# The first stage of a hybrid decoder step: conditioning weights in whole rows, and a shift that is added apart

## The chip, the cores and the metric

The kernel runs on one core of a Trainium2 chip. The metric is the device time of one execution in microseconds (us); a shorter time is better. The engines of the core are named as in the profile: PE is TensorE (PEld its weight loads), DVE is VectorE, ACT is ScalarE, POOL is GpSimd, SP is SyncE, which issues most DMAs.

## What is computed

The reference is one inference step of a one-layer decoder trunk with width 1024, for a prompt of 512 tokens and 8 sample sequences of one token each. The 520 tokens are columns of one batch. What concerns the first stage:

```python
cs = silu(c)                                    # 9 conditioning vectors: prompt, 8 samples
mod = cs @ w_mod + b_mod                        # (9, 6 * 1024)
sh1, sc1, g1, sh2, sc2, g2 = split(mod, 6)
h = rmsnorm(x, norm1_g) * (1 + sc1) + sh1
u = h @ w_in                                    # 1024 x 8192
qa, fa, ia, oga, xb, yb, ga, gb = split(u)
...                                             # HGRN2 heads, RG-LRU, merge, w_out, MLP, final norm
```

Each token's scale and shift depend on its conditioning vector: one for all 512 prompt tokens, one for each sample. All is float32.

## The kernel before

Activations lie transposed: `h` is 8 tiles (k = 0 to 7) of 128 features by 520 tokens. To keep float32 accuracy, each matrix product is made from three fast products: an operand is split into a high part (a rounding copy, on ACT) and a low part (the rest, a subtraction on DVE), and PE adds high x high, high x low, low x high. One weight tile of 1024 x 128 is thus 8 (k) x 3 x 2 (halves of 260 tokens) = 48 products in `products` (L115). `gemm` makes them, `take_w` fetches the tile: it keeps loads (`_load_w`, L66, buffers "wst", four of them) and splits (`_split_w`, L75 and L78) some tiles ahead. Float32 products without a split (w_mod's, for instance) stand as two passes in the trace.

`run` lists the weight tiles in order. Head 0 of the HGRN2 part needs four: f, q, g and v (kf, kq, kg, kv). The first two are multiplied in `begin`, which is the first stage; the rest follow in `head`.

`begin` loads the conditioning vectors and x (L393, 512 KB for 128 tokens, rows of 4 KB). It then loads w_mod's scale and shift columns for each k as one tile "wm" of 1024 x 256 (L1432, two loads of 512 KB each, in runs of 512 B). The first two weight tiles go between. For each k, `mod` multiplies the 9 conditioning vectors with that tile (L356, in four groups of 32 columns of the array), copies the result out (L358), turns it (L372), and adds up the groups and the bias (L376, L380) into `modT`. `norm_x` and `scale_x` normalise x by rows; `transposed` turns 128 features at a time (L426) and ACT puts the result back (L427). `affine_split` forms `h[k]`, with scale and shift at once: the high part on ACT (L447), the full value and the low part on DVE (L448, L449), the samples on POOL (L443 to L445). Products of the f and q tiles with `h[k]` follow as each k is ready.

Small parameters are loaded as rows and turned by PE: `transpose_in` takes a tile "ps" in PSUM (the memory that PE writes to), transposes into it (L222), and DVE copies it out (L223). There are two "ps" tiles. `parameters_mod_in` does one such turn, `parameters_in` four.

The order of instructions on an engine is made by a scheduler at build time, from priorities (the order in the code) and estimated times: an instruction whose inputs or buffer aren't ready can be passed by a later one. `behind` and `issue_after` add an order by hand, with no wait of their own. At run time each engine takes its instructions in the order so fixed.

Of the kernel before, what the change touches and what calls it, by code (L numbers as in the profile page):

```python
# [6 lines left out]
F32 = mybir.dt.float32  # L7
# [26 lines left out]
LEAD = 4  # L34
# [13 lines left out]

class Kernel:
    def __init__(self, ctx, tc, ins, outs):  # L50
        self.ctx, self.tc, self.nc = ctx, tc, tc.nc
        self.i, self.o = ins, outs
        self.group, self.sigmoids, self.mod_open = None, [], None
        self.ppt_free = True
# [14 lines left out]
    def _split_w(self, st, place, after=None):  # L69
# [6 lines left out]
        if after:  # L76
            self.behind(ins, after)
# [9 lines left out]
    def load_split(self, key, stage):  # L87
        return self._split_w(self._load_w(key, stage), self.split_place())

    def take_w(self, key):  # L90
# [7 lines left out]
        while self.wnext_split < min(last + 1, len(self.wspecs)):  # L98
            while self.wnext_load < min(self.wnext_split + LOADS, len(self.wspecs)):
                self.wstage[self.wnext_load] = self._load_w(self.wspecs[self.wnext_load], self.wst)  # L100
                self.wnext_load += 1
# [4 lines left out]
        self.wcur += 1  # L106
        return self.wsplit.pop(n)

    def products(self, ps, w, a, first, last, extra=0, halves=(0, 1), after=None):

        (wh, wl), (ah, al) = w, a
        for n, (x, y) in enumerate(((wh, ah), (wh, al), (wl, ah))):
            for s in halves:
                c = slice(s * HALF, (s + 1) * HALF + s * extra)
                self.last_product = self.nc.tensor.matmul(ps[:, s, :c.stop - c.start], x, y[:, c],  # L115
# [4 lines left out]
    def gemm(self, keys, acts, extra=0):  # L120

        ps = self.pmm.tile([128, 2, 512], F32, name="mm")
        for q, key in enumerate(keys):
            hi, lo = self.take_w(key)
            for k in range(KO):
                n = q * KO + k
                self.products(ps, (hi[:, k], lo[:, k]), acts[n], n == 0, n == len(keys) * KO - 1, extra)
                if self.mod_open and k == MODK:
                    self.mod_close(self.last_product)
# [52 lines left out]
    def identity(self):  # L182
        nc, sb = self.nc, self.consts
        jp = self.start.tile([128, 128], I32, name="pi")
        nc.gpsimd.iota(jp, pattern=[[1, 128]], base=0, channel_multiplier=-1)
        self.ident = sb.tile([128, 128], F32, name="ident")
        nc.vector.tensor_scalar(self.ident, jp, 0.0, None, OP.is_equal)
        one = self.start.tile([128, 128], F32, name="ti")
# [6 lines left out]
    def constants(self):  # L195
        nc, sb = self.nc, self.hc

        pi = self.start.tile([128, NC, 32], I32, name="pi")
        ti = self.start.tile([128, NC, 32], I32, name="ti")
        nc.gpsimd.iota(pi, pattern=[[0, NC], [0, 32]], base=0, channel_multiplier=1)  # L200
        nc.gpsimd.iota(ti, pattern=[[0, NC], [1, 32]], base=0, channel_multiplier=0)
# [26 lines left out]
    def bounds(self):  # L228

        nc = self.nc  # L230
        r = self.start.tile([16, 128], F32, name="ra")
        nc.gpsimd.dma_start(r[0:8], self.rows8(self.i["hg_lower"]))
        nc.gpsimd.dma_start(r[8:16], self.rows8(self.i["lru_lambda"]))
# [11 lines left out]
        nc.scalar.activation(e, e, AF.Exp)  # L245
        self.exps = nc.scalar.activation(ex, na, AF.Exp)
# [6 lines left out]
        self.decay = ex, s, s2, acc, d  # L253

    def decays(self):

        nc = self.nc
        ex, s, s2, acc, d = self.decay
# [13 lines left out]
    def parameters_mod(self):  # L272

        r = self.start.tile([64, 128], F32, name="ra")
        for a, b, name in ((0, 48, "b_mod"), (48, 56, "norm1_g"), (56, 64, "norm2_g")):
            self.nc.sync.dma_start(r[a:b], self.rows8(self.i[name]))
# [70 lines left out]
    def mod(self, keys, w=None):  # L347
# [3 lines left out]
        w = w or self.take_w(self.mod_key(*keys[0]))  # L351
# [6 lines left out]
        first = nc.scalar.copy(ev[:, :n], ps[:, :n])  # L358
        self.mod_open = ev, keys
        if self.ppt_free:  # L360
            self.mod_close()
        return first

    def mod_close(self, after=None):
# [4 lines left out]
        pool, name = (self.ppt, "pt") if self.ppt_free else (self.pps, "ps")  # L369
        pt = pool.tile([128, 512], F32, name=name)  # L370
        for j in range(len(keys)):
            ins = nc.tensor.transpose(pt[:, j * 128:(j + 1) * 128], ev[:, j * 128:(j + 1) * 128], self.ident)  # L372
            if after:
                self.behind(ins, after)
# [3 lines left out]
        for j, (part, k) in enumerate(keys):  # L378
            g = (self.n1g if part == 1 else self.n2g)[:, k:k + 1] if part in (1, 4) else None
# [14 lines left out]

    def norm_x(self):
        nc = self.nc
        ss = self.sm.tile([128, 16], F32, name="ss")
        nc.vector.memset(ss, 1.0)
        junk = lambda: self.pmm.tile([128, 2, 512], F32, name="mm").rearrange("p a b -> p (a b)")
        j = junk()  # L400
        nc.vector.tensor_tensor(j[:NB], self.xsn, self.xsn, OP.mult)
        nc.vector.tensor_reduce(ss[:NB, NC:NC + 1], j[:NB], mybir.AxisListType.X, OP.add)
        for t in range(NC):
            last = nc.scalar.activation(junk(), self.xn[:, t], AF.Square, accum_out=ss[:, t:t + 1])
        self.behind(nc.scalar.activation(self.act0, self.act0, AF.Sigmoid), last)
        ss = ss[:, 0:8]
        nc.vector.tensor_scalar(ss, ss, 1.0 / D, EPS, OP.mult, OP.add)
        self.rs1 = self.rsqrt_small(ss, 8)

# [10 lines left out]
    def transposed(self, k):  # L420

        nc = self.nc
        ps = self.ppb.tile([128, 512], F32, name="pb")
        x = self.xn[:, :, k * 128:(k + 1) * 128]
        for t in range(NC):
            nc.tensor.transpose(ps[:, t * 128:(t + 1) * 128], x[:, t], self.ident)  # L426
        nc.scalar.copy(x, ps.rearrange("p (t f) -> p t f", f=128))  # L427
        return x

    def transposed_s(self):  # L430
# [4 lines left out]
        return ps  # L435
# [1104 lines left out]
```

## Time and profile before

| what | value |
|---|---|
| time, median of three runs | 1045.49 us (1044.67 to 1045.71) |
| the profiled execution's own time | 1044.54 us |
| its span, first to last instruction | 1042.6 us |
| PE, PEld | 1005.1 us, 968.5 us busy (96%, 93%) |
| DVE, ACT, POOL | 694.9, 526.1, 112.8 us busy |
| mean granted clock of TensorE | 0.996 |
| loads by SP's queue (hardware queue) | 130.28 MB, 44.1% of 16 engines' span |

The span is what the profile covers; the execution's own time is 1.94 us more. Busy time is the union of an engine's instructions. Windows give the busy time of each engine in a stretch, with the granted clock, the share in which the 16 DMA engines were busy, and GB/s. The chain of waits follows the work that ended last back to what released it.

### The profile page before, as it was taken

Reading aid. Unit: us, or ns where it says so; the run is one execution under the profiler, and the core shown is the slowest. Engines: PE = TensorE matmul, PEld = TensorE weight load, DVE = VectorE, ACT = ScalarE, POOL = GpSimd, SP = SyncE. Lnnn points to the kernel's source line nnn. Section 1 sums busy time; section 2 is a strip of 40 time slices with the busy share of each in tenths; the row PEclk is TensorE's granted clock in tenths of the full one; section 3 lists DMA queues with packets and bytes.
Section 4 is the critical chain, followed back from the end, with each engine's and each line's share of the span. In section 5 each row is a group of like instructions: output and inputs, shape, how many; then the busy total and the mean of one; then the engine's idle time right before and its main releaser. Section 6 shows DMA issues by size and latency. Waiting matters only on the chain.

```text
span 1042.6 us, 24269 instructions
## 1 busy us (share of the span) xinstructions
PE 1005.1 (96%) x9940; PEld 968.5 (93%) x9940; DVE 694.9 (67%) x1583; ACT 526.1 (50%) x1020; POOL 112.8 (11%) x215
## 2 busy tenths in 40 slices
PE   2999999999999999999999999999999999999995
PEld 1799999999999999989999999999999999999994
DVE  7558688695867768465333337767767676777775
ACT  5445753573574456342122224366555655656653
POOL 2200000000000000020000000011422231232040
PEclk9999999999999999999999999999999999999998
DMA  9963344343434324496555578332572484274242
GB/s 277 260 178 107 110 134 115 112 136 114 126 116 126 113 82 135 137 312 178 163 157 157 157 217 234 93 97 67 124 181 70 100 174 125 52 158 96 62 81 83
DMA packets 247792, 143.71 MB, mean 138 GB/s; under 512 B 6622, under 2 KB 242326, under 8 KB 247674
## 3 DMA queue, kind: packets, MB, share of 16 engines
q1 hardware_dynamic: 237874, 130.28, 44.1%
q0 software_dynamic: 9808, 11.89, 6.3%
q8 instruction: 78, 1.28, 0.5%
q14 instruction: 32, 0.26, 0.1%
HBM read 123.61 MB, written 11.26 MB: 129 GB/s over the span
## 4 chain that ended last, share of the span: by engine, by line
PE 90%; DMA 3%; SPq 3%; ACT 1%; DVE 1%; issue 1%; DVEq 0%; ACTq 0%
PE mm L115 65%; PE ps L1085 8%; PE pt L1085 4%; PE pb L1085 2%; PE ps L356 2%; SPq L1432 2%; PE pb L702 1%; PE ps L561 1%; DMA wst<-in_w_branch_a_dram 1%; DMA wst<-in_w_in_dram 1%; DMA wm<-in_w_mod_dram 1%; PE mm L1085 1%; PE pt L645 1%; PE pt L634 1%; PE ps L529 1%
## 5 line engine op out<-in xcount | busy, mean ns | idle before, releaser
L115 PE MATMUL mm<-h,whi 128*128 128x260 f32 (+1 forms) x3072 | 513.9, 286 | 1.4 <-ACT X L137 1.4
L115 PEld LDWEIGHTS mm<-h,whi 128*128 128x128 f32 x3072 | 427.3, 188 | 7.0 <-issue 3.4
L115 PE MATMUL mm<-h,wlo 128*128 128x260 f32 (+1 forms) x1536 | 316.4, 285 | 0.0
L75 ACT CAST whi<-wst 128x1024 fp32r<-128x1024 f32 x168 | 175.8, 1048 | 228.9 <-PE mm L115 175.4
L78 DVE TENSOR_TENSOR wlo<-wst,whi 128x1024 fp32r<-128x1024 f32 x168 | 205.1, 1222 | 91.2 <-ACT whi L75 90.1
L115 PEld LDWEIGHTS mm<-h,wlo 128*128 128x128 f32 x1536 | 240.0, 189 | 1.5 <-issue 1.0
L115 PE MATMUL mm<-a,whi 128*128 128x260 f32 x512 | 84.6, 285 | 0.0
L115 PEld LDWEIGHTS mm<-a,whi 128*128 128x128 f32 x512 | 70.6, 188 | 1.4 <-issue 1.4
L115 PE MATMUL mm<-a,wlo 128*128 128x260 f32 x256 | 52.3, 284 | 0.0
L797 POOL DMA_DIRECT2D t<-oaT_d x8 | 4.3, 550 | 399.2 <-ACT ma L137 389.0
L1181 DVE TENSOR_TENSOR f<-f 128x260 f32<-128x260 f32 x64 | 27.3, 427 | 28.3 <-ACT f L1176 27.6
L1170 ACT ACTIVATE ft<-ft,fsh 128x512 f32<-128x512 f32 (+2 forms) x36 | 24.0, 676 | 36.0 <-DVE ft L1167 36.0
L115 PE MATMUL mm<-b,whi 128*128 128x260 f32 x256 | 41.8, 285 | 0.0
L1173 POOL TENSOR_TENSOR ft<-ft,fsh 128x8 f32<-128x8 f32 x28 | 17.6, 629 | 219.0 <-DVE ft L1167 219.0
L115 PEld LDWEIGHTS mm<-a,wlo 128*128 128x128 f32 x256 | 39.5, 188 | 0.2 <-issue 0.2
L115 PEld LDWEIGHTS mm<-b,whi 128*128 128x128 f32 x256 | 35.0, 188 | 1.6 <-issue 1.6
L1215 POOL DMA_DIRECT2D ma<-snap x28 | 27.2, 971 | 35.2 <-issue 30.9
L1197 POOL DMA_DIRECT2D ma<-snap x28 | 26.2, 935 | 43.6 <-DMA ma<-snap 28.1
L813 DVE TENSOR_TENSOR t<-mm,t 128x520 f32<-128x520 f32 x8 | 5.6, 700 | 36.7 <-PE ps L372 36.7
L1176 ACT ACTIVATE f<-ft 128x520 f32<-128x520 f32 (+1 forms) x36 | 20.8, 587 | 14.4 <-POOL ft L1174 12.3
L376 DVE TENSOR_REDUCE mods<-ps 128x9 f32<-128x36 f32 x32 | 6.1, 192 | 31.4 <-PE ps L372 31.3
L115 PE MATMUL mm<-b,wlo 128*128 128x260 f32 x128 | 25.9, 283 | 0.0
(488 smaller groups left out, 1876.4 us busy)
## 6 DMA issues: line engine op xcount, KB each, us to landing
wst<-in_w_in_dram SPq DMA_DIRECT2D x64, 512.0 KB
wst<-in_w_mod_dram SPq DMA_DIRECT2D x32, 512.0 KB
wst<-in_w_ff_dram SPq DMA_DIRECT2D x64, 256.0 KB
wst<-in_w_ff_dram SPq DMA_DIRECT2D x32, 512.0 KB
wm<-in_w_mod_dram SPq DMA_DIRECT2D x16, 512.0 KB
st<-in_state_hgrn_dram SPq DMA_DIRECT2D x8, 512.0 KB
vb<-vd SPq DMA_DIRECT2D x8, 512.0 KB
out_dram<-st SPq DMA_DIRECT2D x8, 512.0 KB
```

Source lines behind the costliest of these rows:

```text
L75: ins = self.nc.scalar.copy(hi, st)
L78: self.nc.vector.tensor_tensor(lo, st, hi.bitcast(F32), OP.subtract)
L115: self.last_product = self.nc.tensor.matmul(ps[:, s, :c.stop - c.start], x, y[:, c], start=first and n == 0, stop=last and n == 2)
L356: nc.tensor.matmul(ps[r:r + 32, :n], self.cT[:, k, :], w[:, k, :], start=k < 4, stop=k >= KO - 4)
L1085: ins = self.nc.tensor.matmul(ps, x[:, w], y[:, f], start=j in (1, 7, 2) and k == 0 and n == 0, stop=k == 3 and n == 2, skip_group_check=True)
L1170: nc.scalar.activation(t[:, :p], t[:, :p], AF.Relu, bias=sh[:, 0:1])
L1173: eng.tensor_tensor(t[:, p:], t[:, p:], sh[:, 1:9], OP.add)
L1176: nc.scalar.activation(f, self.two(self.ft)[:, a:a + n], AF.Square)
L1181: self.nc.vector.tensor_tensor(f[:, n], f[:, a], f[:, b], op)
L1197: nc.gpsimd.dma_start(x[1][:, b], v[:, :n], accum_op=OP.add)
L1215: nc.gpsimd.dma_start(x[t][:, a], s[p], accum_op=OP.add)
L1432: nc.sync.dma_start(raw[k][:, :, j * 128:(j + 1) * 128], w[r:r + 1024, c:c + 128].rearrange("(k p) n -> p k n", p=128))
```

## The change

It concerns `begin` and what it calls; the stages behind it keep their code.

- w_mod is loaded in whole rows: `load_rows` takes 128 rows of 1024 columns (4 KB each), first the eight row tiles of the scale, later the eight of the shift in the same eight buffers. `mod_rows` adds up the conditioning product of each row tile in one PSUM tile, `mod_out` copies it out, `mod_cols` turns it and adds the bias, for all eight k at once.
- The first three weight tiles of head 0 (f, q, g) are loaded and split in `begin`, in buffers of their own, and multiplied with `h` as scaled only, without the shift (`scaled`, `rest`).
- The shift's share of these three tiles, shift x weights for 9 conditioning vectors, is a small product (`pw`), which is split (`shw`) and added to the three sums by a product with an indicator matrix (`shifted`, `indicator`): 9 rows spread to 520 tokens. Afterwards `h` is formed a second time, with the shift (`again`), for all later tiles.
- While `begin` runs, each instruction on PE, ACT and DVE is chained behind the one before it on its engine (`InOrder`), so that these three engines follow the order of the code. SP and POOL are not chained.
- `ready_w(1, 1)` loads and splits the v tile's weights before the products, and v's product goes to the PSUM tiles "pt" and "pb". Later weight splits stand behind the last of `again` on ACT (`start_act`).
- The loads of b_mod and the norm weights move from SP's to POOL's queue; the iotas and small parameter loads move ahead.

```diff
--- before.py
+++ after.py
-LEAD = 4
+FIRSTS = 3
...
+class InOrder:
...
+        def __getattr__(self, name):
+            fn = getattr(self.engine, name)
+            def call(*a, **kw):
+                ins = fn(*a, **kw)
+                if self.last:
+                    self.tc.add_manual_dep(ins.ins, self.last.ins.name, NOSYNC, reason="order")
+                self.last = ins
+                return ins
+            return call
...
-        if after:
-            self.behind(ins, after)
+        if after or self.start_act:
+            self.behind(ins, after or self.start_act)
...
+    def ready_w(self, end, loads=LOADS):
+        while self.wnext_split < min(end, len(self.wspecs)):
+            while self.wnext_load < min(self.wnext_split + loads, len(self.wspecs)):
                 self.wstage[self.wnext_load] = self._load_w(self.wspecs[self.wnext_load], self.wst)
                 self.wnext_load += 1
             st = self.wstage.pop(self.wnext_split)
             spec = self.wspecs[self.wnext_split]
             self.wsplit[self.wnext_split] = st if WHOLE in spec else self._split_w(st, self.split_place())
             self.wnext_split += 1
...
+        r = self.start.tile([64, 128], F32, name="rm")
         for a, b, name in ((0, 48, "b_mod"), (48, 56, "norm1_g"), (56, 64, "norm2_g")):
-            self.nc.sync.dma_start(r[a:b], self.rows8(self.i[name]))
+            self.nc.gpsimd.dma_start(r[a:b], self.rows8(self.i[name]))
         return r
...
+    def load_rows(self, part, k, t=None):
+        t = t or self.start.tile([128, D], F32, name="wm", bufs=NWM)
+        self.nc.sync.dma_start(t, self.i["w_mod"][0, k * 128:(k + 1) * 128, part * D:(part + 1) * D])
+        return t
+    def mod_rows(self, ps, k, w):
+        for j in range(4):
+            self.nc.tensor.matmul(ps[32 * j:32 * j + 32, :256], self.cT[:, k, :], w[:, 256 * j:256 * j + 256],
+                                  start=k == 0, stop=k == KO - 1)
+    def mod_out(self, ps):
+        ev = self.sm.tile([128, 256], F32, name="modev")
+        self.nc.scalar.copy(ev, ps[:, :256])
+        return ev
+    def mod_cols(self, part, out, ev, scale=None):
+        nc = self.nc
+        pt = self.ppb.tile([128, 512], F32, name="pb")
+        own = self.ident.rearrange("p (j c) -> p j c", c=32)[:, :, :NM]
+        for h in range(2):
+            nc.tensor.matmul(pt[:, 64 * h:64 * h + 4 * NM].rearrange("p (j b) -> p j b", b=NM),
+                             ev[:, 128 * h:128 * h + 128], own, start=True, stop=True)
+        src = pt[:, :128].rearrange("p (h x) -> p h x", h=2)[:, :, :4 * NM].rearrange("p h (j b) -> p h j b", b=NM)
+        out = out.rearrange("p (j h) b -> p h j b", h=2)
+        col = lambda c: c.rearrange("p (j h) -> p h j", h=2)[:, :, :, None].to_broadcast([128, 2, 4, NM])
+        nc.vector.tensor_tensor(out, src, col(self.bmod[:, part * 8:part * 8 + 8]), OP.add)
+        if scale is not None:
+            nc.vector.tensor_tensor(out, out, col(scale), OP.mult)
...
-        return nc.vector.tensor_tensor(lo, f, hi.bitcast(F32), OP.subtract)
+        hi, x = self.h[k][0], self.xcols(k)
+        f = self.start.tile([128, L], F32, name="ht", bufs=2)
+        if shift:
+            ins = nc.scalar.activation(v(hi), x, AF.Identity, bias=sh, scale=sc)
+            nc.vector.tensor_scalar(v(f), x, sc, sh, OP.mult, OP.add)
+        else:
+            ins = nc.scalar.activation(v(hi), x, AF.Copy, scale=sc)
+            nc.vector.tensor_scalar(v(f), x, sc, None, OP.mult)
+        return k, f, ins
+    def rest(self, t):
+        (hi, lo), f = self.h[t[0]], t[1]
+        return self.nc.vector.tensor_tensor(lo[:, :L], f, hi[:, :L].bitcast(F32), OP.subtract)
...
+            parts = list(zip((self.two(og)[:, s] for s in range(2)), first[2]))
+        else:
+            parts = [(self.two(og), self.gemm(kg, self.h)[:, :, :HALF])]
         with self.urgent():
-            self.sigmoid(self.two(og), ps)
...
-        ps = self.gemm(kv, self.h)[:, :, :HALF]
         v = self.slot(self.hg, "e")
+        if first:
+            ps = self.gemm(kv, self.h, ps=[self.ppt.tile([128, 512], F32, name="pt"),
+                                           self.ppb.tile([128, 512], F32, name="pb")], after=self.last_product)
+            parts = [(self.two(v)[:, s], ps[s][:, :HALF]) for s in range(2)]
+        else:
...
             kf, kq, kv, kg = self.head_cols(h)
-            steps.append(([kf, kq, kg, kv][2 if h == 0 else 0:], self.head_start if h == 0 else self.head, h))
+            steps.append(([kf, kq, kg, kv][FIRSTS if h == 0 else 0:], self.head_start if h == 0 else self.head, h))
...
     def begin(self):
...
+        plain = self.nc
+        nc = self.nc = InOrder(self.tc)
         self.start = self.open_pool("start", 1)
+        mm = lambda: self.pmm.tile([128, 2, 512], F32, name="mm")
...
+        rb, rm, par = self.load_bounds(), self.parameters_mod(), self.parameters()
+        rows = [self.start.tile([128, D], F32, name="wm", bufs=NWM) for _ in range(KO)]
         self.load_x()
+        keys = [self.head_cols(0)[j] for j in (0, 1, 3)]
+        raw = [self._load_w(keys[0], self.wst)]
+        rows = [self.load_rows(1, k, t) for k, t in enumerate(rows)]
+        raw += [self._load_w(key, self.wst) for key in keys[1:]]
+        first = []
+        def split_first(n):
+            hi, lo = (self.start.tile([128, KO, 128], F32R, name=x, bufs=FIRSTS) for x in ("fhi", "flo"))
+            nc.scalar.copy(hi, raw[n])
+            first.append((hi, lo))
+        def split_rest(n):
+            hi, lo = first[n]
+            nc.vector.tensor_tensor(lo, raw[n], hi.bitcast(F32), OP.subtract)
+        self.constants()
         self.cond()
...
+        self.norm_samples()
+        self.bounds(rb)
+        last = self.norm_x()
+        self.exponentials()
+        self.behind(nc.scalar.activation(self.act0, self.act0, AF.Sigmoid), last)
+        split_first(0)
+        self.scale_x()
+        self.shp = self.start.tile([128, KO, 32], F32, name="shp")
+        nc.vector.memset(self.shp, 0.0)
         hi, lo = (self.act.tile([128, KO, T2], F32R, tag="h", name="h", bufs=2) for _ in range(2))
         self.h = [(hi[:, k, :T], lo[:, k, :T]) for k in range(KO)]
...
+        psc = self.ppt.tile([128, 512], F32, name="pt")
+        for k in range(4):
+            self.mod_rows(psc, k, rows[k])
+        split_rest(0)
+        self.parameters_mod_in(rm)
+        t = self.transposed(0, 2, mm())
+        self.put_back(nc.scalar.copy, t)
+        self.mod_rows(psc, 4, rows[4])
+        t = self.transposed(2, 2, mm())
+        self.put_back(nc.vector.tensor_copy, t)
+        self.mod_rows(psc, 5, rows[5])
+        xs = self.transposed_s()
+        t = self.transposed(4, 1, ps()[:, None])
+        self.put_back(nc.scalar.copy, t)
+        self.mod_rows(psc, 6, rows[6])
+        t = self.transposed(5, 1, ps()[:, None])
+        self.put_back(nc.vector.tensor_copy, t)
+        self.mod_rows(psc, 7, rows[7])
+        ev = self.mod_out(psc)
+        last_x = [self.transposed(6, 1, ps()[:, None])]
+        self.mod_cols(1, self.modT[:, 8:16], ev, self.n1g)
+        last_x.append(self.transposed(7, 1, ps()[:, None]))
+        rows = [self.load_rows(0, k) for k in range(KO)]
+        fs = self.start.tile([128, KO, NB], F32, name="fs")
+        t = self.scaled(0)
+        nc.vector.tensor_tensor(fs, xs, self.modT[:, 8:16, 1:9], OP.mult)
+        nc.vector.tensor_copy(hi[:, :, L:T], fs)
+        nc.vector.tensor_tensor(lo[:, :, L:T], fs, hi[:, :, L:T].bitcast(F32), OP.subtract)
+        self.rest(t)
+        split_first(1)
+        t = self.scaled(1)
+        split_rest(1)
+        self.rest(t)
+        split_first(2)
+        for x in last_x:
+            self.put_back(nc.scalar.copy, x)
+        t = self.scaled(2)
+        split_rest(2)
+        self.rest(t)
+        for k in range(3, KO):
+            self.rest(self.scaled(k))
+        self.indicator()
+        self.ready_w(1, 1)
         self.parameters_in(*par)
...
+        self.decays()
+        self.first = [mm()[:, :, :HALF], mm()[:, :, :HALF], [ps()[:, :HALF], ps()[:, :HALF]]]
+        acc = [[x[:, s] for s in range(2)] for x in self.first[:2]] + [self.first[2]]
+        def products(n, *ks):
+            wh, wl = first[n]
+            for k in ks:
+                ah, al = self.h[k]
+                for m, (x, y) in enumerate(((wh, ah), (wh, al), (wl, ah))):
+                    for s in range(2):
+                        nc.tensor.matmul(acc[n][s], x[:, k], y[:, s * HALF:(s + 1) * HALF], start=k == 0 and m == 0,
+                                         stop=n < 2 and k == KO - 1 and m == 2)
+        def shifted(n):
+            for m, x in enumerate(shw):
+                for s in range(2):
+                    nc.tensor.matmul(acc[n][s], x[:, n * 128:(n + 1) * 128], self.ind[:, s * HALF:(s + 1) * HALF],
+                                     start=False, stop=n == 2 and m == 1)
+        def again(*ks):
+            for k in ks:
+                t = self.scaled(k, True)
+                plain.gpsimd.tensor_copy(hi[:, k, L:T], fs[:, k])
+                plain.gpsimd.tensor_tensor(lo[:, k, L:T], fs[:, k], hi[:, k, L:T].bitcast(F32), OP.subtract)
+                self.split_last, self.start_act = self.rest(t), t[2]
+        for k in (0, 1):
+            products(0, k)
+            products(1, k)
+        products(2, 0, 1)
+        for k in (2, 3):
+            for n in range(FIRSTS):
+                products(n, k)
+        psh = self.ppt.tile([128, 512], F32, name="pt")
+        for k in range(4):
+            self.mod_rows(psh, k, rows[k])
+        for n in range(FIRSTS):
+            products(n, 4)
+        for k in range(4, KO):
+            self.mod_rows(psh, k, rows[k])
+        ev = self.mod_out(psh)
+        for n in range(FIRSTS):
+            products(n, 5)
+        self.mod_cols(0, self.shp[:, :, :NM], ev)
+        plain.gpsimd.tensor_tensor(fs, fs, self.shp[:, :, 1:9], OP.add)
+        again(0, 1, 2)
+        products(0, 6)
+        products(1, 6)
+        pw = self.ppt.tile([128, 512], F32, name="pt")
+        for n in range(FIRSTS):
+            for k in range(KO):
+                r = 32 * (k % 4)
+                nc.tensor.matmul(pw[r:r + 32, n * 128:(n + 1) * 128], self.shp[:, k, :], raw[n][:, k, :],
+                                 start=k < 4, stop=k >= KO - 4)
+        shw = [self.start.tile([128, FIRSTS * 128], F32R, name=f"shw{x}") for x in "hl"]
+        nc.scalar.copy(shw[0], pw[:, :FIRSTS * 128])
+        nc.vector.tensor_tensor(shw[1], pw[:, :FIRSTS * 128], shw[0].bitcast(F32), OP.subtract)
+        products(2, 6, 7)
+        shifted(0)
+        products(0, 7)
+        shifted(1)
+        products(1, 7)
+        shifted(2)
+        again(*range(3, KO))
+        self.last_product = nc.tensor.last
+        self.nc = plain
...
+        _, _, p, n = self.counts
+        nc.vector.tensor_scalar(p, p, 31, None, OP.bitwise_and)
+        b = self.start.tile([128, 1], F32, name="ind_b")
+        nc.vector.tensor_copy(b, p)
+        self.ind = self.start.tile([128, T], F32R, name="ind")
+        nc.vector.tensor_scalar(self.ind, n, 0.0, b, OP.max, OP.is_equal)
...
```

206 lines of the change are left out of this document (91 added, 115 removed).

## The prediction

> **What bounds the kernel now.** I read the page first (busy shares and slices), then the windows of the first 60 us, then the chain of waits through them, then the engines' own order of instructions there.
>
> ```profile
> span 1042.6 us, 24269 instructions
> PE 1005.1 (96%) x9940; PEld 968.5 (93%) x9940; DVE 694.9 (67%) x1583; ACT 526.1 (50%) x1020; POOL 112.8 (11%) x215
> ```
>
> TensorE (PE) is busy for all but 37.5 us of the span. The windows (busy us and instructions of PE, PEld, DVE, ACT, POOL; granted clock; DMA share; GB/s) say where those are:
>
> ```profile
> 0.00:10.00 10.00, 1.24 (x9) 1.10 (x9) 6.28 (x33) 5.42 (x12) 6.50 (x17) 1.00 0.75 257
> 10.00:20.00 10.00, 2.97 (x20) 1.24 (x20) 6.86 (x40) 4.42 (x7) 0.00 (x0) 1.00 1.19 290
> 20.00:30.00 10.00, 6.55 (x67) 3.78 (x69) 5.87 (x20) 7.38 (x12) 0.00 (x0) 1.00 1.21 289
> 30.00:40.00 10.00, 8.47 (x94) 6.34 (x86) 6.68 (x16) 5.35 (x10) 4.24 (x15) 1.00 1.21 291
> 54.27:60.13 5.86, 5.86 (x48) 5.86 (x49) 5.76 (x18) 4.35 (x12) 0.00 (x0) 1.00 1.07 287
> 60.13:100.00 39.87, 39.87 (x492) 38.19 (x491) 29.32 (x77) 17.61 (x35) 0.00 (x0) 1.00 0.37 108
> ...
> 4.00:9.00 5.00, 0.48 (x4) 0.31 (x3) 4.24 (x19) 3.42 (x8) 3.45 (x8) 1.00 1.01 391
> ```
>
> In the first 40 us PE idles 20.8 us (40 less 1.24, 2.97, 6.55 and 8.47) while the DMA share is at or over 1 from 10 us on: the stage is bound by loads. From 54.27 on PE runs without a gap. The last row is the one stretch in which the queue moves mainly x, in rows of 4 KB: 391 GB/s against 290 in the stretches that load weight tiles in runs of 512 B. The chain of waits (start, us, what) names the same thing:
>
> ```profile
> 29.16 7.62 DMA wm<-in_w_mod_dram
> 36.78 0.14 issue
> 36.91 1.07 PE ps L356 x16
> ...
> 53.62 0.61 ACT X L137
> 54.23 0.04 issue
> 54.27 15.62 PE mm L115 x128
> ```
>
> So the place to compare is the end of the third weight tile of head 0 (its gate column, kg), after which either kernel goes on with the same work (kv, rg_x, ...) on a full PE. A 128x260 product costs 15.62 / 128 = 0.122 us there, and the third tile's 48 end at 54.27 + 48 x 0.122 = **60.1**: the 48 instructions of the window row that ends at 60.13. What the change is worth is the shift of this point.
>
> **The change, part by part.** The loads come first. x is seen complete by the last Square (9.95, below). Behind it now lie one weight tile, 0.52 MB at 290 GB/s = 1.8 us, and the eight scale rows, 4.19 MB. Nothing in the trace loads w_mod by rows; the x row bounds it from above (391 GB/s, 10.7 us), the tile rows from below (290, 14.5 us). I take 391, since a row here is the same 128 runs of 4 KB. The last scale row lands at 9.95 + 1.8 + 10.7 = 22.5.
>
> ```profile
> 9.95 1.03 ACT L404 ACTIVATE mm<-xn 128x1024 f32<-128x1024 f32 x1 [0.48 <-DMA xn<-in_x_prompt_dram]
> 26.98 0.37 ACT L358 COPY modev<-ps 128x256 f32<-128x256 f32 x1 [0.36 <-PE ps L356]
> 28.05 0.23 DVE L376 TENSOR_REDUCE mods<-pt 128x18 f32<-128x72 f32 x1 [2.15 <-PE pt L372]
> 28.32 0.42 DVE L380 TENSOR_SCALAR modT<-mods,pm 128x9 f32<-128x9 f32 x2
> 41.29 0.38 PE L372 MATMUL pt<-ident,modev 128*128 128x128 f32 x2
> 49.24 0.42 DVE L380 TENSOR_SCALAR modT<-mods,pm 128x9 f32<-128x9 f32 x2
> ```
>
> Its four products are 8 passes, half of 1.07 us; evacuation, turn and addition take 28.74 - 26.98 = 1.76 as above (the new form drops the reduce and adds a wider pass; bounds 1.4 to 2). All scales stand at **24.8**, where before the last column's scale came at 49.66 by the same steps. So far the change gains much.
>
> What decides is the order. Every PE, ACT and DVE instruction of the new begin() is chained to the one before on its engine. After the two transposes 6 and 7 and the turn of the scales, PE's next instructions are the four transposes of parameters_in, and only then the first product. They write to "ps" tiles, of which there are two. The third needs the first one's copy on DVE. That copy stands in DVE's order behind all eight scaled/rest pairs, the indicator, and the low half of the kv weight (ready_w). So the third transpose waits for all of that, and every product waits behind it on PE, though h[0] is ready early. The trace shows both halves of this: the transposes of these parameters, at present spread between products with their copies right behind, and products' predecessors held up by one such transpose:
>
> ```profile
> 16.95 0.34 PE L222 MATMUL ps<-ident,ra 64*128 64x64 f32 x1 [9.91 <-DMA ra<-in_norm_g_dram]
> 17.21 1.93 PE L356 MATMUL ps<-wm,cT 128*32 128x256 f32 x16
> 20.45 1.27 PE L356 MATMUL ps<-wm,cT 128*32 128x256 f32 x16
> 25.85 1.07 PE L356 MATMUL ps<-wm,cT 128*32 128x256 f32 x16 [1.20 <-DMA wm<-in_w_mod_dram]
> ...
> 45.61 0.27 PE L222 MATMUL ps<-ident,rb 57*128 57x57 f32 x1
> 49.34 0.27 PE L222 MATMUL ps<-ident,rc 64*128 64x64 f32 x1
> 51.14 0.25 PE L222 MATMUL ps<-ident,rd 96*128 96x96 f32 x1
> ```
>
> PE stood 9.91 us at the transpose of 16.95, and the first w_mod products followed it at once.
>
> DVE's work from 24.8 to that copy, by these rows (in the first two, two back to back):
>
> ```profile
> 32.57 1.30 DVE L449 TENSOR_TENSOR h<-ht,h 128x520 fp32r<-128x520 f32 x2
> 33.79 0.99 DVE L448 TENSOR_SCALAR ht<-xn,modT 128x512 f32<-128x512 f32 x2
> ...
> 45.91 0.22 DVE L223 COPY pa<-ps 128x57 f32<-128x57 f32 x1
> 53.25 1.23 DVE L78 TENSOR_TENSOR wlo<-wst,whi 128x1024 fp32r<-128x1024 f32 x1 [1.57 <-ACT whi L75]
> 54.40 0.55 DVE L470 TENSOR_SCALAR e<-e,lb,lbf 128x520 f32<-128x520 f32 x1
> ```
>
> Eight pairs at 0.50 + 0.65 = 9.2; two low halves of first tiles 2.4; three sample instructions 0.7 (as the copy); the indicator, like the 128x520 TENSOR_SCALAR plus two small, 0.7; the kv low half 1.2; the copies of the first two parameters 0.4. Sum 14.6; starts overlap ends by up to 0.1, so 14.4 (bounds 13 and 14.6). ACT's own part (eight scalings, two splits, two put-backs) hides beside it:
>
> ```profile
> L447 ACT ACTIVATE h<-xn,modT 128x512 fp32r<-128x512 f32 x8 | 6.5, 816 | 8.5 <-DVE modT L380 8.5
> L427 ACT COPY xn<-pb 128x512 f32<-128x512 f32 x8 | 4.7, 583 | 3.2 <-PE pb L426 3.2
> L75 ACT CAST whi<-wst 128x1024 fp32r<-128x1024 f32 x3 | 3.1, 1045 | 5.5 <-DMA wst<-in_w_in_dram 3.9 <-PE mm L115 1.6
> ```
>
> that is 6.5 + 2.1 + 1.2 = 9.8 us, plus 1.05 for the kv high half, behind which ACT has nothing to do until PE's products. The kv load must have landed by some 35 us. Its buffer is free from the start (four in the pool, three taken), while each shift row waits until its scale row has been used, so I expect it on SP's queue ahead of most shift rows: 22.5 + 3 x 1.8 (q, g, kv) = 28. With a last 0.2 for the transposes, products begin at 24.8 + 14.4 + 0.2 = **39.4**. The four weight and eight shift loads have landed by 22.5 + 5.4 + 10.7 = 38.6, so nothing later waits for them.
>
> PE then has: 144 products x 0.122 = 17.6; the shift rows, 64 passes, 4 x 1.07 = 4.3; pw, 24 calls or 48 passes of 128 columns, no row like it: half of a 256-column pass (1.07/16/2) gives 1.6, a whole one 3.2, I take 1.6 because the columns halve; 12 indicator products 1.5; the shift's turn, as at 41.29, 0.4. Sum **25.3**. The waits inside are covered: the shift's evacuation by the 18 products of k=5 (2.2 us), shw's two halves (about 1.1) by the 12 of products(2,6,7) (1.5), the second scaling of h[3..7] (5 x 1.15 on DVE) by the last 24 instructions and kv's first 18; without that cover kv would wait up to 2 us.
>
> A burst after idling costs more: 16 passes took 1.93 at 17.21, 1.27 at 20.45 and 1.07 later, at a granted clock of 1.00 in those windows. New products would start after some 13 us of idle PE, so I add 0.86 + 0.20 = 1.1 (bounds 0 and 2.2, twice that).
>
> [...]
>
> The rest moves at no price.
>
> ```profile
> 0.83 0.23 POOL L185 IOTA pi<- 128x128 int32 x1 [0.40 <-POOLq L1521]
> 2.67 0.53 POOL L293 DMA_DIRECT2D rb<-in_hg_onorm_g_dram  x1
> ```
>
> b_mod and the two norm vectors go from SP to POOL's queue ahead of the seven parameter loads, and four more iotas go ahead of them all: 3 x 0.53 + 4 x 0.23 = 2.5 us later on POOL, whose loads are wanted only near 17 us and later. In return SP loses their three issues. The 16 w_mod loads stay 16, with fewer and longer runs. The third tile's split is taken from later. Sixteen small POOL instructions rewrite the sample columns beside PE's work. The wait at 54.27 for two sigmoids goes, since kv writes to ppt and ppb; the comparison at 60.1 contains that already.
>
> The third tile ends at 39.4 + 25.3 + 1.1 = **65.8** against 60.1: **5.7 us later**, after which PE is full as before. The profiled execution has 1044.54 (span 1042.6 and 1.9 around it) and becomes 1050.2; it stands 0.95 under the median 1045.49, so the median becomes **1051.2**. Break-even: products would have to start at 33.7.
>
> **Rivals.** *Products aren't held* (the other side). If the parameter copies come out ahead of the scaling on DVE, whatever orders them so, products start with h[0] at about 26.5, follow DVE to h[2] (24.8 + 3 x 1.15 + 2.4 + 0.7 = 31.4, 36 products by then), and have 108 x 0.122 + 4.3 + 1.6 + 1.5 + 0.4 = 21.0 left: third tile at 52.4, 7.7 us earlier, 1037.8. For it speaks that the scales are ready 25 us earlier; against it the written order and two ps tiles. It decides where the first product stands before 33.7.
>
> *The kv tile comes last in SP's queue.* It lands at 38.6; high half 1.05, low half 1.2, copies 0.4 put the products at 41.5: 2.1 later, 1053.3. It decides only if more than about five shift rows go first; against it stands its free buffer.
>
> *Whole rows load no faster*: 14.5 instead of 10.7, all later by 3.8: 1055.0. Against it stands the x row.
>
> *The hold is there but short*: x lands 1.1 earlier without w_mod tiles in between, DVE takes 13, no slow burst: 5.7 - 1.1 - 1.4 - 1.1 = 2.1 later or less, 1047.6.
>
> **How the numbers follow.** About 0.2% (2.1 us) is what a measurement of this kernel can tell from no change. Chances: held as summed 0.54, kv last 0.12, slow rows 0.06, held but short 0.12, not held 0.16. Faster 0.16; the short hold gives most of "same", 0.11; slower 0.73. The likeliest case's own range is 1047.6 to 1056 (its lower bounds together; pw 1.6 and a slow burst 1.1 more, and a kv stall of 2). The range for 8 in 10 reaches down through "same" to 1043.5 and up to 1056.5, leaving out the free-running case.
>
> **What would show it.** In the changed profile: a gap on PE ending in parameters_in's third transpose with the DVE copy as releaser, products starting at 37 to 42 with h[0] written by 27; the scale rows at about 390 GB/s, and modT before 26; 20 to 27 us of nearly full PE from the first product to the end of kg. A first product before 33, or a PE gap that ends in a load, would prove it wrong.

## The result, and the profile after

The changed kernel takes 1056.73 us (median of 4 runs, 1055.04 to 1061.14), the one before 1045.08 on the same chip: ratio 1.0118, 95% interval 1.0086 to 1.0150. It is 11.7 us slower, where 5.7 were forecast. The direction and the gap on PE came as predicted; the size is outside the range.

The page of the changed kernel (its profiled execution took 1056.08 us), then its windows with the columns shown before:

```profile
span 1054.2 us, 24378 instructions
PE 1010.7 (96%) x9992; PEld 972.5 (92%) x9992; DVE 704.7 (67%) x1589; ACT 526.2 (50%) x1021; POOL 113.7 (11%) x213
```

```profile
10.00:20.00 10.00, 5.51 (x38) 1.98 (x39) 7.97 (x28) 8.50 (x15) 0.70 (x2) 1.00 1.05 383
...
30.00:40.00 10.00, 0.72 (x2) 0.36 (x2) 9.48 (x16) 6.97 (x11) 0.00 (x0) 0.60 0.81 322
40.00:45.00 5.00, 2.72 (x13) 2.72 (x14) 4.20 (x20) 0.00 (x0) 0.00 (x0) 0.50 0.27 77
```

From 10 to 20 us, when mainly rows are loaded, 383 GB/s move, where the tiles ran at 290. Then PE stands still: 0.72 us of work in the ten from 30 to 40, while DVE is busy for 9.48 of them. The granted clock falls to 0.60 and 0.50. PE's own order shows what stands at both ends of the gap (all lines that begin() issues through the chain bear the line number of its wrapper, L68, so the tile names tell them apart):

```profile
14.74 1.08 PE L68 MATMUL pt<-wm,cT 128*32 128x256 f32 x8 [0.63 <-DMA wm<-in_w_mod_dram]
16.45 1.08 PE L68 MATMUL pt<-wm,cT 128*32 128x256 f32 x8 [0.63 <-DMA wm<-in_w_mod_dram]
17.74 1.08 PE L68 MATMUL pt<-wm,cT 128*32 128x256 f32 x8 [0.20 <-DMA wm<-in_w_mod_dram]
...
19.04 1.97 PE L68 MATMUL mm<-ident,xn 128*128 128x128 f32 x8
...
21.84 1.09 PE L68 MATMUL mm<-ident,xn 128*128 128x128 f32 x8
...
25.76 0.64 PE L68 MATMUL pt<-wm,cT 128*32 128x256 f32 x8
...
31.92 0.35 PE L68 MATMUL ps<-ident,rb 57*128 57x57 f32 x1 [3.92 <-ACT xn L68]
32.40 0.37 PE L68 MATMUL ps<-ident,rc 64*128 64x64 f32 x1
42.28 0.58 PE L68 MATMUL ps<-ident,rd 96*128 96x96 f32 x2 [9.52 <-DVE pa L68]
42.57 1.22 PE L68 MATMUL mm<-h,fhi 128*128 128x260 f32 x4
...
46.87 0.65 PE L68 MATMUL ps<-h,fhi 128*128 128x260 f32 x4
...
52.74 1.93 PE L68 MATMUL pt<-wm,cT 128*32 128x256 f32 x32
...
63.04 1.52 PE L68 MATMUL pt<-wst,shp 128*32 128x128 f32 x48
...
69.22 0.28 PE L143 MATMUL pt<-h,whi 128*128 128x260 f32 x1
```

PE first waits 3.92 us until ACT has emptied a "ps" tile of x (xn); then the two turns of rb and rc run, the turns of rd wait 9.52 us for the DVE copy "pa", and the first product follows at 42.57. The third tile ends where kv's first product starts, at **69.2** (60.1 before). DVE's order up to that copy:

```profile
27.84 0.23 DVE L68 TENSOR_TENSOR modT<-modT,pm 128x72 f32<-128x72 f32 x1
...
29.20 0.69 DVE L68 TENSOR_TENSOR h<-ht,h 128x512 fp32r<-128x512 f32 x1
...
39.42 0.69 DVE L68 TENSOR_TENSOR h<-ht,h 128x512 fp32r<-128x512 f32 x1
...
40.88 1.22 DVE L68 TENSOR_TENSOR wlo<-wst,whi 128x1024 fp32r<-128x1024 f32 x1
42.02 0.21 DVE L68 COPY pa<-ps 128x57 f32<-128x57 f32 x1
```

h[0] is whole at 29.9, 12.7 us before its first product. The kv load went ahead of the shift rows on SP, and ACT rounded its tile at 35.93 without a wait:

```profile
12.91 10.54 SPq L93 DMA_DIRECT2D wst<-in_w_in_dram  x3
23.56 6.70 SPq L389 DMA_DIRECT2D wm<-in_w_mod_dram  x8
```

### The profile page after: what moved, and what is told of

Read it like the earlier page. It is cut to its first block, busy times and chain, and to the rows that moved or that the text cites. A ratio compares the mean times of both kernels' runs of the same rounds, so it can differ in the third digit from the quotient of the medians.

```text
span 1054.2 us, 24378 instructions
## 1 busy us (share of the span) xinstructions
PE 1010.7 (96%) x9992; PEld 972.5 (92%) x9992; DVE 704.7 (67%) x1589; ACT 526.2 (50%) x1021; POOL 113.7 (11%) x213
## 3 DMA queue, kind: packets, MB, share of 16 engines
q1 hardware_dynamic: 223442, 130.24, 42.2%
## 4 chain that ended last, share of the span: by engine, by line
PE 88%; DMA 5%; DVE 4%; ACT 1%; issue 1%; SPq 1%; DVEq 0%; ACTq 0%
PE mm L143 60%; PE ps L1177 8%; PE pt L1177 4%; PE pb L1177 2%; PE ps L427 2%; PE mm L68 1%; PE pb L794 1%; DMA wst<-in_w_branch_a_dram 1%; PE ps L653 1%; DMA wm<-in_w_mod_dram 1%; DMA vb<-vd 1%; DMA wst<-in_w_in_dram 1%; PE ps L68 1%; DVE h L68 1%; PE mm L1177 1%
## 5 line engine op out<-in xcount | busy, mean ns | idle before, releaser
L143 PE MATMUL mm<-h,whi 128*128 128x260 f32 (+1 forms) x2944 | 490.2, 285 | 0.4 <-ACT X L166 0.4
L143 PEld LDWEIGHTS mm<-h,whi 128*128 128x128 f32 x2944 | 409.3, 188 | 4.7 <-issue 3.2
L143 PE MATMUL mm<-h,wlo 128*128 128x260 f32 x1472 | 305.4, 286 | 0.8 <-DVE wlo L105 0.8
L102 ACT CAST whi<-wst 128x1024 fp32r<-128x1024 f32 x164 | 171.7, 1049 | 215.0 <-PE mm L143 172.0
L105 DVE TENSOR_TENSOR wlo<-wst,whi 128x1024 fp32r<-128x1024 f32 x164 | 200.1, 1220 | 82.1 <-ACT whi L102 81.7
L143 PEld LDWEIGHTS mm<-h,wlo 128*128 128x128 f32 x1472 | 230.3, 189 | 2.8 <-DVE wlo L105 1.2
L614 ACT ACTIVATE st<-st,fkq 128x128 f32<-128x128 f32 x64 | 20.3, 391 | 14.4 <-DVE fkq L593 13.0
L442 DVE TENSOR_REDUCE mods<-ps 128x9 f32<-128x36 f32 x32 | 6.1, 190 | 31.7 <-PE ps L439 31.6
```

The lines of the kernel that those rows point to most:

```text
L102: ins = self.nc.scalar.copy(hi, st)
L105: self.nc.vector.tensor_tensor(lo, st, hi.bitcast(F32), OP.subtract)
L143: self.last_product = self.nc.tensor.matmul(ps[s][:, :c.stop - c.start], x, y[:, c], start=first and n == 0, stop=last and n == 2)
L614: nc.scalar.activation(st[:, b], st[:, b], AF.Copy, scale=fkq[:, 0, b:b + 1])
```

## The experiments

All were run against the kernel before; "third tile" is the start of kv's first product. The short diffs are against the changed kernel unless another is named.

**e1: the parameters' turns early.**

```diff
         self.parameters_mod_in(rm)
+        self.parameters_in(*par)
         t = self.transposed(0, 2, mm())
...
         self.ready_w(1, 1)
-        self.parameters_in(*par)
```

> The changed kernel with one line moved: the four turns of parameters_in come right after parameters_mod_in, so that no product stands behind a copy at the end of DVE's first pass. Theory (the hold): products begin at about 29.5 us instead of 42.6, follow DVE up to h[2], and the third tile ends near 55 us instead of 69.3; the time falls by about 14 us from 1056.7 to some 1042.5, below the 1045.1 of the kernel before. Rival A (the added work and the two rounds of loads are what costs): the gap on PE reappears ahead of the shift's rows or the weight splits, and the time stays above 1053. Rival B (the cold clock is most of the loss): products still start early but the gain is 5 us or less.

Measured: 1043.76 us, ratio to the kernel before 0.9987 (0.9976 to 0.9999): 13.0 us less than the changed kernel, by one moved line. PE of e1:

```profile
20.81 1.92 PE L68 MATMUL mm<-ident,xn 128*128 128x128 f32 x8
...
23.67 1.97 PE L68 MATMUL mm<-ident,xn 128*128 128x128 f32 x8
...
31.64 0.53 PE L68 MATMUL mm<-h,fhi 128*128 128x260 f32 x2 [0.94 <-ACT h L68]
...
59.13 0.28 PE L143 MATMUL pt<-h,whi 128*128 128x260 f32 x1
```

Products begin at 31.6 and the third tile ends at 59.1. The hold is shown to be the cause; rivals A and B fall. The start missed the forecast 29.5 by 2.1, because the turns now stand ahead of x's and both eights of x's turns took 1.9 us, where the second took 1.1 in the changed kernel. The third tile missed the forecast 55 by 4.1. Some 1.7 of that is the clock, an estimate from two windows (5 x 0.27 + 5 x 0.08 = 1.75): PE waits 0.94 and 0.48 us at its first products, and the granted clock is 0.73 from 30 to 35 us and 0.92 from 35 to 40.

**e4: the turns ahead of the indicator and the kv split only.**

```diff
+        self.parameters_in(*par)
         self.indicator()
         self.ready_w(1, 1)
-        self.parameters_in(*par)
```

> The changed kernel with parameters_in put ahead of the indicator and of the v tile's split, still behind all eight scalings. Theory (the place of the copy in DVE's order sets the start): products begin 2.0 us earlier, at 40.6 (0.6 of indicator work and 1.2 of the low half go from ahead of the copy), and the time falls by 2 us to 1054.7. Rival (something else ends the wait at the same time, the v tile's load or the scalings themselves being read by the first products): the start stays at 42 or moves by less than 0.5.

Measured: 1053.57 us (1050.98 to 1058.73), ratio 1.0087 (1.0065 to 1.0110). PE of e4:

```profile
40.32 0.58 PE L68 MATMUL ps<-ident,rd 96*128 96x96 f32 x2 [7.54 <-DVE pa L68]
40.61 1.22 PE L68 MATMUL mm<-h,fhi 128*128 128x260 f32 x4
```

The start moved by 1.96, as the work taken from ahead of the copy says. The place of that copy in DVE's order sets the start one for one. The third tile came only 1.1 earlier, at 68.1: the granted clock is 0.50 from 40 to 45 us here too, so that the products which start earlier run slowly for longer. The time fell by 3.2 instead of 2.0, with runs too far apart to read the difference.

**e5: one PSUM tile for the four turns**, in the place where the change has them.

```diff
-        self.transpose_in(pa, ra, 57)
-        self.transpose_in(pb, rb, 64)
...
+        ps = self.ppb.tile([128, 512], F32, name="pb")
+        c = 0
+        for out, rows, n in ((pa, ra, 57), (pb, rb, 64), (pc[:, :96], rc[:, 0, :], 96), (pc[:, 96:], rc[:, 1, :], 96)):
+            nc.tensor.transpose(ps[:, c:c + n], rows[:n, :], self.ident[:n, :n])
+            c += n
+        c = 0
+        for out, n in ((pa, 57), (pb, 64), (pc, 192)):
+            nc.vector.tensor_copy(out, ps[:, c:c + n])
+            c += n
```

> The changed kernel with parameters_in where the change has it, but its four turns written side by side into one PSUM tile (pb), from which three DVE copies read: PE no longer has to wait for a copy between the turns. Theory (two ps tiles are what ties PE to the end of DVE's order): the turns take 1 us, products begin at 29.5 to 30, the third tile ends at about 57, 2 us ahead of the kernel with the turns put early (59.1), whose scales came 2.3 us late; the time is about 1041.5. Rival (the place of the instructions in the order matters, not the tiles): products still begin after 40 and the time stays above 1052.

Measured: 1041.37 us, ratio 0.9966 (0.9954 to 0.9979). PE of e5:

```profile
29.44 0.53 PE L68 MATMUL mm<-h,fhi 128*128 128x260 f32 x2 [0.36 <-ACT h L68]
...
56.21 0.28 PE L143 MATMUL pt<-h,whi 128*128 128x260 f32 x1
```

The order is the change's own, and DVE is no earlier: its last addition for the scales starts at 28.34, where the changed kernel has it at 27.84 and copies "pa" 14.2 us later, so that here "pa" comes near 42.5 (an estimate). Only the buffer is different, and PE goes on at once. So it is the second use of a "ps" tile that tied PE to the end of DVE's list. The place of the turns does no harm without that tie; with it, moving them is a cure too (e1).

**e3: no chain.**

```diff
                 ins = fn(*a, **kw)
-                if self.last:
-                    self.tc.add_manual_dep(ins.ins, self.last.ins.name, NOSYNC, reason="order")
                 self.last = ins
```

> The changed kernel without the chain of instructions on PE, ACT and DVE: the scheduler orders them. In its order on PE the products no longer stand behind all four parameter transposes and all scaling. Theory (the order is the cause): products begin before 33 us, the third tile ends between 55 and 62 us, and the time lies between 1042 and 1050. Rival A (loads and added work): it stays above 1053.

Measured: 1051.32 us, ratio 1.0060 (1.0047 to 1.0074); just outside the expectation. PE of e3:

```profile
31.18 0.51 PE L68 MATMUL mm<-h,fhi 128*128 128x260 f32 x2 [0.35 <-ACT h L68]
...
56.78 0.74 PE L68 MATMUL mm<-ind,shwh 128*128 128x260 f32 x4 [2.02 <-ACT shwh L68]
...
58.45 0.80 PE L68 MATMUL mm<-ind,shwl 128*128 128x260 f32 x2 [0.69 <-DVE shwl L68]
...
61.99 0.28 PE L141 MATMUL pt<-h,whi 128*128 128x260 f32 x1
```

Without the chain the products begin at 31.2, so the hold goes. But the scheduler spends the products that should cover the shift's split before it is due: PE waits 2.02 and 0.69 us there, the granted clock falls to 0.79 from 55 to 60 us, and the third tile ends at 62.0. That is 1.9 us behind the kernel before; the time is 6.3 behind, and the rest, which arises after begin(), no run isolates. The chain as such is no fault; one call in it stood at the wrong place for its buffers.

**e2 and e7: PE kept busy through the gap.** Transposes of the identity that nobody reads go ahead of the parameters' turns, 80 in e2 and 122 in e7.

```diff
         self.ready_w(1, 1)
+        warm = self.ppt.tile([128, 512], F32, name="pt")
+        for _ in range(122):
+            nc.tensor.transpose(warm[:, :128], self.ident, self.ident)
         self.parameters_in(*par)
```

> The changed kernel with 80 transposes of the identity into a PSUM tile that nobody reads, put on PE ahead of the parameter transposes, so that PE is busy through most of the gap from 28 to 42 us. Theory (the hold, with a slow start of some 1.5 us): products still begin at 42.6, their first 24 take about 2.9 us instead of 4.2, the granted clock of 42 to 46 us is 1.00, and the time falls by 1 to 2 us to about 1055. Rival B (the cold clock is most of what the prediction missed, 6 us, and of the spread over runs): the time falls by 4 us or more to 1052 and the runs lie closer together. If the clock had no part, nothing changes.

> The changed kernel with 122 idle transposes in place of the 80 of the earlier run, so that the gap on PE is covered up to the copy at 42 us (the 80 ended at 37.3, and the products were slow all the same: 24 in 3.9 us). Theory (a slow start after idling costs what the first products show): granted clock 1.00 from 40 to 45, the first 24 products in 2.9 us, and a time 1.3 us under the run with 80, near 1053.3. Rival (the gain of the 80 came from elsewhere, the later order of the scheduler): same time as with 80, 1054.6.

Measured: e2 1054.57 us, ratio 1.0088 (1.0075 to 1.0101); e7 1053.35 us, ratio 1.0081 (1.0066 to 1.0095). A window and PE's order of e2, then the same two of e7:

```profile
40.00:45.00 5.00, 2.16 (x10) 2.16 (x11) 4.31 (x17) 0.00 (x0) 0.00 (x0) 0.50 0.14 40
```

```profile
42.84 0.58 PE L68 MATMUL ps<-ident,rd 96*128 96x96 f32 x2 [5.30 <-DVE pa L68]
43.13 1.21 PE L68 MATMUL mm<-h,fhi 128*128 128x260 f32 x4
...
47.77 0.65 PE L68 MATMUL ps<-h,fhi 128*128 128x260 f32 x4
```

```profile
40.00:45.00 5.00, 4.28 (x37) 3.98 (x35) 4.29 (x21) 0.00 (x0) 0.00 (x0) 1.00 0.30 88
```

```profile
42.41 0.72 PE L68 MATMUL mm<-h,fhi 128*128 128x260 f32 x4
...
45.36 0.64 PE L68 MATMUL ps<-h,fhi 128*128 128x260 f32 x4
...
67.68 0.28 PE L143 MATMUL pt<-h,whi 128*128 128x260 f32 x1
```

80 were too few: PE idled 5.30 us again behind them, the clock stood at 0.50, and the first 24 products took 47.77 - 43.13 = 4.64 us, no less than without them (the 3.9 in e7's expectation counts 18 of them). Whatever brought e2's time down by 2.2 us, it was not a faster start; the intervals of e2 and the changed kernel overlap, so it may be chance. With 122 the clock stays at 1.00 and the first 24 products take 45.36 - 42.41 = 2.95 us instead of 46.87 - 42.57 = 4.30. The slow start costs 1.4 us here (1.35) and no more; rival B falls. The time of e7 against e2 (1.2 less) agrees, but their intervals overlap.

**e6: one tile, and PE kept busy while it waits for the first row tiles** (on top of e5; run again as e10 beside e9).

```diff
+        busy(22)
         last = self.norm_x()
...
         for k in range(4):
+            if k:
+                busy(7)
             self.mod_rows(psc, k, rows[k])
```

Here busy(n) issues n transposes of the identity into a "pb" tile.

> As the kernel with one tile for the turns, with 22 + 3 x 7 transposes of the identity into a PSUM tile that nobody reads, on PE while it waits for the first four row tiles. Theory (PE's slow state, not the last row's landing, makes the scales late: 28.05 where 24.8 was forecast): the eight transposes at 19 us take 1.1 instead of 2.0, eight passes of a row tile 0.6 instead of 1.1, the scales stand 1.5 us earlier, the time is about 1040, and the runs lie closer together. Rival (the rows land late): PE waits for row tiles after 21 us and the scales stand where they did.

> The kernel e6 once more, unchanged, on the same chip as the one with short runs, to compare with. Both theories: 1040 to 1041.5.

Measured: 1040.87 us, ratio 0.9957 (0.9945 to 0.9969); again, 1041.63 (1039.06 to 1046.30), ratio 0.9969 (0.9958 to 0.9981). PE's order of e6, then DVE's:

```profile
18.85 1.09 PE L68 MATMUL mm<-ident,xn 128*128 128x128 f32 x8
...
54.31 0.28 PE L143 MATMUL pt<-h,whi 128*128 128x260 f32 x1
```

```profile
26.43 0.23 DVE L68 TENSOR_TENSOR modT<-modT,pm 128x72 f32<-128x72 f32 x1
```

x's turns take 1.09 us instead of 1.97, and the third tile ends at 54.3, 1.9 before e5. In the time the two can't be told apart, nor do e6's runs lie closer together when there are many. It and e5 beat both kernels.

**e9: w_mod in short runs** (on top of e6): each row tile in two loads with runs of 512 B, its columns permuted, read back in order by the products.

```diff
-        self.nc.sync.dma_start(t, self.i["w_mod"][0, k * 128:(k + 1) * 128, part * D:(part + 1) * D])
+        src = self.i["w_mod"][0, k * 128:(k + 1) * 128, part * D:(part + 1) * D]
+        for a in range(2):
+            self.nc.sync.dma_start(t.rearrange("p (a b n) -> p a b n", a=2, b=4)[:, a],
+                                   src.rearrange("p (b a n) -> p a b n", a=2, b=4)[:, a])
```

> As the kernel with one tile for the turns and PE kept busy (e6), but each row tile of w_mod is loaded by two DMAs in runs of 512 B, as the tiles were before, with its columns permuted on the way and read back in order by the products. It measures what whole rows bring. Theory (rate of runs): the loads from 10 to 20 us go at 290 GB/s instead of 383, the last scale row lands near 26 instead of 22 to 23, the scales stand some 2.5 us later and the time is 2 to 3 us above e6. Rival (PE's own work, not the loads, sets the scales): less than 1 us.

Measured: 1044.57 us, ratio 1.0006 (0.9992 to 1.0021), against e10's 1041.63 on the same chip. A window and DVE's order of e9, then the same two of e10:

```profile
10.00:20.00 10.00, 7.34 (x66) 5.26 (x68) 7.75 (x25) 8.52 (x15) 0.80 (x2) 1.00 1.20 287
```

```profile
29.77 0.23 DVE L68 TENSOR_TENSOR modT<-modT,pm 128x72 f32<-128x72 f32 x1
```

```profile
10.00:20.00 10.00, 9.28 (x78) 6.62 (x76) 7.97 (x28) 8.50 (x15) 1.14 (x2) 1.00 1.05 381
```

```profile
26.63 0.23 DVE L68 TENSOR_TENSOR modT<-modT,pm 128x72 f32<-128x72 f32 x1
```

Whole rows are worth 3.1 us at the scales and 2.9 us in the time, the whole of what e6 wins over the kernel before to within the intervals. In e9 PE does wait for the last row, until 27.71 (26 was expected); in e6, of which e10 is a second run, it takes up the last row at 24.36 without a wait.

**e8: the shift's products left out** (on top of e5): without pw, its split and `shifted`.

> As the kernel with one tile for the turns, but the shift's products (pw, its split, the twelve products with the indicator) are left out: f, q and g of head 0 lack the shift's share, so less is computed. It measures what adding the shift apart costs. Theory: PE time alone, 1.5 + 1.5 = 3.0 us less. Rival (it is covered or covers other waits): less than 1.5 us, since PE then waits for the second scaling of h.

Measured: 1040.41 us, ratio 0.9961 (0.9947 to 0.9975). PE of e8:

```profile
52.83 0.28 PE L143 MATMUL pt<-h,whi 128*128 128x260 f32 x1
...
57.76 0.39 PE L143 MATMUL pt<-h,whi 128*128 128x260 f32 x1 [0.94 <-DVE h L68]
```

The third tile ends 3.4 us sooner than in e5, but kv then waits for the second h, 0.94 us at one place and 1.5 in all. In the time 1.0 us is left, which the overlapping intervals don't tell from none: the theory's 3.0 is wrong, the rival nearer. PE's work for the shift also covers DVE's second pass.

## Why the prediction was wrong

The mechanism is right. The turn of rd waits for the copy "pa" behind all scalings, the indicator and the kv low half; the products wait behind the turn; h[0] is there 12.7 us earlier. e1, e4 and e5 show it by three separate ways of loosening it. The rival that stands on free products gives 1037.8; e5, which frees them, measured 1041.4. Of the signs that the prediction named, the gap, its releaser and the full PE behind it came; the times did not: products began at 42.6, not by 42, h[0] was written at 29.9, not by 27, and modT at 28.1, not before 26.

Term by term:

- *The last scale row at 22.5*: 1.1 too early. No instruction waited for a row after 17.74, but the trace records when a load has landed, in 16 signals for each: the last of this row's came at 23.62. From the landing of the weight tile ahead of them (11.49) the eight rows took 12.1 us where 10.7 were summed.
- *All scales at 24.8*: **this is the term that failed.** They stood at 28.1 (27.84 + 0.23). The sum let PE take up the last row as it landed, at 22.5. It landed 1.1 later, and PE took it up only at 25.76, another 2.1 later; from there to the scales it took 2.3 us, as summed. PE was behind: x's 32 turns and the later row tiles stand in one order with it, x was scaled only at 18.6, and PE ran slowly up to some 21.8 us (8 passes 1.08, later 0.64; 8 turns 1.97, later 1.09). From 17.74 to the end of the scales' turn at 27.5 the PE rows have no wait worth naming. e6, where PE is kept busy, takes up its last row at 24.36. So 1.4 of the 2.1 goes with the slow state, and 0.7 is work that stood ahead of the last row on PE. All this is read from one execution of each kernel.
- *DVE 14.4 to the copy*: 28.1 to 42.2, 14.1.
- *Turns 0.2*: products began 0.35 after the copy. Start 42.6 against 39.4.
- *PE 25.3 and 1.1*: 69.2 - 42.6 = 26.6 against 26.4. Shift rows 3.9 (4.3 forecast), pw 1.5 (1.6), slow start 1.4 by e7 (1.1).
- *Afterwards as before*: the third tile is 9.1 later, the profiled execution 11.5. The sum had nothing for the other 2.4. PE's waits behind the third tile, of the changed kernel and then of e7:

```profile
PE ps L439 <- ACT modev L429: 2.2, 2, 1.1
...
PE mm L143 <- DVE wlo L105: 0.8, 2, 0.6
```

```profile
PE ps L439 <- ACT modev L429: 0.7, 1, 0.7
```

The changed kernel waits 2.2 us for evacuations in the later w_mod steps and 0.8 for a weight split; e7, with the same code behind begin(), waits 0.7 and not at all, and its profiled execution ends 1051.61 - 67.7 = 983.9 behind its third tile, against 986.9 for the changed kernel and 984.4 for the kernel before. The order of instructions is not the reason why these two differ: behind begin(), PE, ACT and DVE carry out the same instructions in the same order in both traces, one for one, and so they do in e4 (the kernel before has another order there). What differs is when a load lands. On ACT the evacuation stands behind the rounding of a weight tile, which waits for that tile. The changed kernel, then e4 in its slowest run (1058.73 us):

```profile
463.00 1.05 ACT L102 CAST whi<-wst 128x1024 fp32r<-128x1024 f32 x1 [4.97 <-DMA wst<-in_w_in_dram]
```

```profile
465.07 1.04 ACT L102 CAST whi<-wst 128x1024 fp32r<-128x1024 f32 x1 [8.11 <-DMA wst<-in_w_in_dram]
```

PE's longest wait for such an evacuation was 1.1 us in the changed kernel and 0.7 in e7. In e4 ACT's wait is 3.1 us longer than in the changed kernel, and the execution ends 1058.73 - 68.1 = 990.6 behind its third tile, 3.7 later. So with one order that time ranges over several us, and the 2.4 is within the spread of the changed kernel's own runs (1055.04 to 1061.14). Whether any of it belongs to the change stays open: no run isolates it.

The kv load came early, as expected. The granted clock was 0.50 from 40 to 45 us, behind the gap, and the slow start cost 1.4 (e7), where the prediction took 1.1 from the rows of the kernel before. The range was too narrow: its upper end added a longer pw, a slower burst and a stall of kv, and held nothing for PE's own work ahead of the last row or for the stages behind begin().

## What to carry to other kernels

When an order is fixed by hand on several engines, look at each buffer that one engine fills and another empties: with two tiles and four uses, the third use waited for the emptying, 9.52 us here, because that stood at the end of the other engine's list. Give such a small job a tile of its own, or place both its halves at the same point of both lists. And when loads get faster, add up the work that the consumer has in its own order ahead of the last one, at the speed which it has after waiting (eight turns of x took 1.97 us, the next eight 1.09): here that made 2.1 of the 3.3 us by which the scales came late. The other 1.1 was the rows' landing.

## What was new about the hardware

In e2 a busy stretch did not carry over the gap behind it. After 80 transposes (8.90 us) PE idled 5.30 us, and the granted clock was 0.50 from 40 to 45 us; with 122 (13.48 us), which left a wait of 0.72 us, it stayed at 1.00. In e1 it was below 1.00 around shorter waits: 0.73 from 30 to 35 us and 0.92 from 35 to 40, with waits of 0.94 and 0.48 us; in e6 it stayed at 1.00 through waits of 0.36, 0.48 and 0.31 us. Nor did sparse work bring PE up in the changed kernel: bursts of 1.08 us between waits of 0.20 to 0.63 us, from 13 to 18 us, left the next eight turns at 1.97 us.

The window of those turns shows a granted clock of 1.00, but that is no measurement: the trace's record of the clock begins only at 21.67 us, at 1.00, just where the turns fall from 1.97 to 1.09 us, and the windows count time without a record as 1.00. The prediction read the kernel before in the same way, whose record begins at 20.92. Ahead of the first record, like instructions tell the state of PE by their durations, as here 1.97 and 1.09 us.
